# A hybrid three-branch encoder layer on one core: first weight loads fenced behind the first pieces' scaling, products placed between states and outputs, and planner holds lengthened

## The chip, the cores and the metric

The kernel runs on one core of one Trainium2 chip. The metric is the device time of one execution in microseconds (us), lower is better; the time before is the median of three executions, 756.55 us (756.28 to 756.60). All times below are microseconds unless marked otherwise. The engines are called PE (TensorE, the matrix engine), DVE (VectorE), ACT (ScalarE), POOL (GpSimd) and SP (SyncE, which here only issues transfers).

## The reference, cut to what matters

One layer reads x (1024 frames of 1024 numbers), normalises each frame, projects it to 16 segments, runs three linear-attention branches of four heads each side by side (HGRN2, GLA, mLSTM), norms and gates each head, and projects the 1536 concatenated columns back, with a residual and a last norm.

```python
def reference(x, norm_w, w_in, b_in, ...):
    h = _rmsnorm(x, norm_w[l])
    parts = _split_columns(h @ w_in[l] + b_in[l])
    y_hg = _gated_head_norm(_hgrn2_branch(parts, lower_bounds[l]), parts["hg_z"], hg_norm_w[l])
    y_gla = _gated_head_norm(_gla_branch(parts, gla_w_a2[l], gla_b_a2[l]), parts["gla_z"], gla_norm_w[l])
    y_ml = _gated_head_norm(_mlstm_branch(parts, ml_conv_w[l], ml_conv_b[l]), parts["ml_z"], ml_norm_w[l])
    y = jnp.concatenate([y_hg, y_gla, y_ml], axis=-1)
    x = x + y @ w_out[l]
    return _rmsnorm(x, final_norm_w)
...
def step(state, inp):            # one chunk of a gated linear attention head
    b = jnp.cumsum(gc, axis=2)
    att = jnp.einsum("bhtd,bhsd,bhtsd->bhts", qc, kc, dec)   # dec: pairwise decays, causal
    out = einsum(att, vc) + einsum(qc * jnp.exp(b), state)
    state = jnp.exp(b_last) * state + einsum(kc * jnp.exp(b_last - b), vc)
```

GLA's decays come from a small second projection: `log_sigmoid(parts["gla_a"] @ w_a2 + b_a2) / 16`. mLSTM's gates are two columns a head, with a running maximum.

## The kernel before

**Arithmetic.** Every product is made in three passes: an operand is split into a high part in a reduced fp32 format and a low remainder, and PE multiplies high by high, low by high, and high by low into the same accumulator bank. Such a triple with 512 moving columns is the unit of the projections (lines 346 to 348). `load_w` (line 220) fetches one block of weights: a transfer on SP into a `wraw` buffer (two of them), the high part by a copy on ACT (line 230, `whi`), the low part by a subtraction on DVE (line 231, `wlo`); both have four buffers.

**Start.** `proj_first` projects the first three pieces (f0, q0, z0 of HGRN2 head 0) in six accumulator banks while x arrives. The frames' scales are applied afterwards: `row_sums` and `row_scale` bring them across with PE transposes, ACT copies them into RSB (line 276), and DVE multiplies the six banks by RSB (line 339), which frees the banks. The next product, the pass over v0 (line 379, 280 columns: v0, the mLSTM gates and the GLA gate input), needs two of these banks. Its outputs are scaled on DVE (line 406).

**The planner.** From there on a class `Weave` interleaves chains (Python generators) with the stream of projections on PE. A chain yields `(cost, delay)` or `(cost, delay, tag, held)`: PE is taken to be busy for `cost`, the chain may go on `delay` later, and the accumulator slot of kind `tag` is taken to be free `held` later. These guesses alone decide where small products stand in PE's order, which is fixed when the program is built; the other engines' orders follow from a scheduler and are fixed too. Each engine works through its queue in order.

**The chains that the change touches.** For each half of a head: `radix4` (line 441, two levels of decays with 48-column products at line 462, copied out of bank `pt` at line 467) and `tree` (lines 491 and 522); then `tail` runs `states` (transposes of K at line 573 to `kd` at 575, four products at 592, and a scan over chunks on DVE at 598, `S`), and `att_out` or `pair_out` (lines 607 to 640). The last row of the first half's output needs the last state of the second half (line 614, 640). `finish_half` squares the outputs on ACT (558), takes a power on POOL (217) and scales them on ACT (561), after which the `po` bank is free. `gates` makes the gate rows and, in `gla_alpha` (line 743), the GLA decays: pairs of products at line 750 into `po` banks, the second pair subtracted on DVE at 768. `ml_chain` (line 897) runs the mLSTM heads: `ml_states` (transposes, products at line 851, scan at 857) and `ml_out` (871 with the attention, 879 with the states).

**Sums.** `sum_steps` (line 1069) adds pairs of blocks of the output weights for a Strassen-like output product, one step after each projected piece: two transfers into the same two `wraw` buffers, an addition on DVE (line 1075), a store. The transfers of `load_w` and of these sums take turns in the two buffers.

Of the kernel before, what the change touches and what calls it, by code (L numbers as in the profile page):

```python
# [10 lines left out]
AF = mybir.ActivationFunctionType  # L11
# [125 lines left out]
def kernel(ctx: ExitStack, tc: tile.TileContext, x, xt, wt, wide, cols, vbias, wa2, wq, fw, masks, sel,  # L137
                      ident_in, out):
    nc = tc.nc
# [9 lines left out]
    po = ctx.enter_context(tc.tile_pool(name="po", bufs=2, space=PS))  # L149
# [10 lines left out]
    RSB = const.tile([128, T], F32, name="RSB")  # L160
# [56 lines left out]
        nc.gpsimd.tensor_tensor(dst, dst, mhalf[:, 0:dst.shape[1]], op=OP.pow)  # L217


    def load_w(src, cuts=None, raw=None, hilo=None):  # L220

        raw = wp.tile([128, 1024], F32, name="wraw", bufs=2) if raw is None else raw
        if hilo is None:
            hilo = [wp.tile([128, 1024], F32R, name=nm, bufs=4) for nm in ("whi", "wlo")]
        hi, lo = hilo

        def part(a, b):
            s = slice(a, b)
            nc.sync.dma_start(raw[:, s], src[:, s])
            nc.scalar.activation(hi[:, s], raw[:, s], AF.Copy)  # L230
            nc.vector.tensor_sub(lo[:, s], raw[:, s], hi[:, s].bitcast(F32))  # L231
        if cuts is None:
            part(0, src.shape[1])
            return hi, lo
        return (hi, lo), [lambda a=a, b=b: part(a, b) for a, b in zip(cuts, cuts[1:])]

# [34 lines left out]
    def row_scale():  # L271
        for half in range(2):
            p = ptr.tile([128, 512], F32, name="tp")
            for j in range(4):
                nc.tensor.transpose(p[:, j * 128:(j + 1) * 128], rs[:, 4 * half + j:4 * half + j + 1].to_broadcast([128, 128]), ident)
            nc.scalar.activation(RSB[:, 512 * half:512 * half + 512], p, AF.Copy)


    wide_w, scales, marks = [], [], []
# [1 line left out]
    def load_wide(i, hilo=None):  # L281
        k0, k1 = KSPLIT[i]
        t = load_w(wide[:, k0 * WIDE:k1 * WIDE], hilo=hilo)
        wide_w.extend((t, k - k0) for k in range(k0, k1))

    def proj_first(pieces):

        ws, loads = [], []
        for i in range(3):
            raw = fp.tile([128, 1024], F32, name="al", bufs=2) if i == 2 else None  # L290
            t, steps = load_w(wt[WIDX[pieces[i][0]]], WCUTS, raw)
            ws.append(t)
            loads.append(steps)
        ps = [[pl.tile([128, 512], F32, name=nm) for _ in range(2)] for pl, nm in ((pmain, "pm"), (po, "po"), (ptree, "pt"))]
        done = [0, 0, 0]

        def matmuls(i, k):
            hi, lo = ws[i]
            for kk in range(done[i], k):
                ks = slice(128 * kk, 128 * kk + 128)  # L300
                for half in range(2):
                    s = slice(512 * half, 512 * half + 512)
                    nc.tensor.matmul(ps[i][half], hi[:, ks], HI[kk][:, s], start=kk == 0, stop=False)
                    nc.tensor.matmul(ps[i][half], lo[:, ks], HI[kk][:, s], start=False, stop=False)
                    nc.tensor.matmul(ps[i][half], hi[:, ks], LO[kk][:, s], start=False, stop=kk == KC - 1)
            done[i] = k
        for k in range(KC):
            if k == 0:
                loads[0][0]()
            build_h(k, 2 if k < 2 else 1)  # L310
            if k == 0:
                loads[1][0]()
                loads[2][0]()
            for i in range(3):
                for a in range(1, len(WCUTS) - 1):
                    if (WORDER[i] + 2 * (a - 1)) == k:
                        loads[i][a]()
            if k >= 3:
                square(k - 3)
            if k < KOUT:  # L320
                for i in range(3):
                    matmuls(i, k + 1)
        for k in range(KC - 3, KC):
            square(k)
        load_wide(0, [fp.tile([128, 1024], F32R, name="al", bufs=2) for _ in range(2)])
        matmuls(0, KC)
        load_wide(1)
        matmuls(1, SUMS)
        mean = row_sums()
        matmuls(1, KC)  # L330
        load_wide(2)
        matmuls(2, SCALE)
        row_scale()
        matmuls(2, KC)
        with tc.issue_after(mean):
            load_consts()
        for (_, dst, evac), pp in zip(pieces, ps):
            for half in range(2):
                nc.vector.tensor_mul(dst(half), pp[half], RSB[:, 512 * half:512 * half + 512])
                evac(half)  # L340

    def nt_half(hi, lo, s):
        p = pmain.tile([128, 512], F32, name="pm")
# [97 lines left out]
    def radix4(Q, K, F, Kc, dA, l4, slack):  # L441

        g = 4 ** l4
        n = 128 // g
        Q4, K4, F4 = (a.rearrange("p (n j g) -> p n j g", j=4, g=g) for a in (Q, K, F))
        P = [F4[:, :, j, g - 1:g] for j in range(4)]
        over = lambda j0, j1: F4[:, :, j0:j1, g - 1:g].to_broadcast([128, n, j1 - j0, g])
        qm = wk.tile([128, 768], F32, name="qm")  # L450
        M = qm.rearrange("p (n j g) -> p n j g", j=6, g=g)
        nc.scalar.activation(qm.rearrange("p (n x) -> p n x", n=n)[:, :, 0:3 * g],
                             Q.rearrange("p (n x) -> p n x", n=n)[:, :, g:4 * g], AF.Copy)
        nc.vector.tensor_tensor(M[:, :, 3:5, :], Q4[:, :, 2:4, :], over(1, 3), op=OP.mult)
        marks.append(nc.vector.tensor_tensor(M[:, :, 5, :], M[:, :, 4, :], P[1].to_broadcast([128, n, g]), op=OP.mult).ins)
        yield 0.0, 4.0 + slack
        yield "pt"
        p = ptree.tile([128, 512], F32, name="pt")
        for c in range(4):
            for a in range(0, 128, 32):  # L460
                q = (4 * c + a // 32) * 48
                nc.tensor.matmul(p[a:a + 32, 48 * c:48 * c + 48], Kc[:, c, a:a + 32], qm[:, q:q + 48], start=True, stop=True)
        pm = p[:, 0:192].rearrange("p (m j g) -> p m j g", j=6, g=g)
        d4 = dA.rearrange("p c (m j g) -> p (c m) j g", j=4, g=g)
        for off, j, w in ((0, 0, 3), (96, 3, 2), (160, 5, 1)):
            mask = mk4[:, l4, off:off + 32 * w].rearrange("p (m j g) -> p m j g", j=w, g=g)
            nc.vector.copy_predicated(d4[:, :, 4 - w:4, :], mask, pm[:, :, j:j + w, :])
        nc.vector.tensor_tensor(Q4[:, :, 1, :], Q4[:, :, 1, :], P[0].to_broadcast([128, n, g]), op=OP.mult)
        nc.vector.tensor_tensor(Q4[:, :, 2:4, :], M[:, :, 3:6:2, :], P[0][:, :, None].to_broadcast([128, n, 2, g]), op=OP.mult)
        nc.vector.tensor_tensor(P[2], P[2], P[3], op=OP.mult)  # L470
        nc.vector.tensor_tensor(P[1], P[1], P[2], op=OP.mult)
        nc.vector.tensor_tensor(K4[:, :, 0:3, :], K4[:, :, 0:3, :], over(1, 4), op=OP.mult)
        marks.append(nc.vector.tensor_tensor(P[3], P[0], P[1], op=OP.mult).ins)
        yield 0.7, 1.9 + slack, "pt", 3.0 + slack

    def tree(Q, K, F, A, dA, nh, half, done, slack=0.0):

# [171 lines left out]
    def tail(w, heads, rows, Q, K, F, V, zs, yi, trees, ready, out_done):  # L649

        yield lambda: ready() and 0 in trees
        S = wk.tile([128, NC, 130], F32, name="S", bufs=1)
        Kc = K.rearrange("p (c t) -> p c t", c=NC)
        states_done, first = [], []
        for half in range(2):
            yield lambda: half in trees
            yield from states(Kc, V[0], F, list(zip(heads, rows)), S, half)
            yield 0.0, 2.2
            states_done.append(half)
            if len(heads) > 1:  # L660
                w.start(pair_out(att, Q, V[0], S, zs, yi, half, states_done, first, out_done))
                continue
            for i, h in enumerate(heads):
                yield lambda: len(zs) > i
                w.start(att_out(h, att[:, (yi + i) % 2], Q[:, i], V[0], S, zs[i], yi + i, half, states_done, first, out_done))
# [77 lines left out]
    def gla_alpha(r, als):  # L743
# [23 lines left out]
                s = slice(512 * half, 512 * half + 512)  # L767
                nc.vector.tensor_sub(al[:, s], ps[half], al[:, s])
        for half in range(2):
            yield 0.0, 0.0, "po", 2.0 + half  # L770
        nc.scalar.activation(al, al, AF.Exp, scale=1.0 / 16.0)
        als.append(al)

# [123 lines left out]
    def ml_chain(w, r, ready, PQK, Vs, ogs, gates, ys, zs, done):  # L897
# [22 lines left out]
        yield lambda: len(gates) == NC  # L920
        yield from ml_states(r, K, E, V, S, 1)
        states_of.append(r)
        yield from ml_out(r, Q, S, V, ogs[0], ys, 1, gates)
        for h in range(2):
            yield lambda: len(zs) > h
            for half in range(2):
                s = slice(512 * half, 512 * half + 512)
                dst = y_tile(4 + h)[:, 1] if r else ys[h]
# [263 lines left out]
    with tc.manual_schedule(engines={mybir.EngineType.PE}):  # L1192
# [87 lines left out]
        for c in range(4):  # L1280
            parts = [R] if c < 3 else [slice(512, 896), last]
            for n, cols in enumerate(parts):
                pc_ = slice(cols.start - 512, cols.stop - 512)
                p = ptree.tile([128, 512], F32, name="pt") if n else pa[c]
# [93 lines left out]
```

## Time and profile before

| | |
|---|---|
| median of three executions | 756.55 us |
| the profiled execution | 757.12 us, of which the core's span is 755.3 us |
| PE | 740.4 us busy, 98% of the span |
| PE weight loads | 619.6 us, under the products |
| DVE | 471.6 us, 62% |
| ACT | 353.2 us, 47% |
| POOL | 60.2 us, 8% |
| transfers | 80.58 MB, mean 107 GB/s |
| granted TensorE clock | 0.995 of full over the span |

PE is busy nearly all the time, so only what PE waits for, or does at the lower clock, can be gained. The list of PE's waits names the line that waited, the line on another engine that ended the wait, the sum, the number of times and the longest. A timeline row is a start, a length, an engine, a line, an operation with its tiles and shapes, a count, and in brackets the idle time ahead of it and what ended that. PE's lengths overlap, so its pace is read from one start to the next.

### The profile page before, as it was taken

The numbers are of one execution on the slowest core, as the hardware profiler recorded it, in microseconds if no ns is written. First come the engines' busy times: TensorE is split into PE (matmuls) and PEld (weight loads), VectorE is DVE, ScalarE is ACT, GpSimd is POOL, SyncE is SP. The second block draws the span as 40 slices with busy tenths as digits, with TensorE's granted clock in tenths as the row PEclk, the third lists the DMA queues.
The fourth block names the chain that finished last, engine by engine and source line by source line (L and its number), as shares of the span: only waits on it lengthen the run. The fifth ranks groups of instructions, "written<-read, shape, count | busy, mean of one in ns | idle before, by whom it ended". The sixth has DMA issues, their size and how long they took to land.

```text
span 755.3 us, 13831 instructions
## 1 busy us (share of the span) xinstructions
PE 740.4 (98%) x5550; PEld 619.6 (82%) x5550; DVE 471.6 (62%) x1004; ACT 353.2 (47%) x772; POOL 60.2 (8%) x107
## 2 busy tenths in 40 slices
PE   9999998999999999999999999999999999999996
PEld 7888886899887899788988878878877878888886
DVE  6987767766467538523662384353564358899864
ACT  6661577842343431544044553345270556454543
POOL 2000130010010020012001200101000110000011
PEclk9999999999999999999999999999999999999998
DMA  8443652332542232102020120031210077543323
GB/s 307 137 154 115 189 183 75 110 91 88 196 146 92 88 137 85 51 29 84 31 85 29 55 84 1 2 126 69 71 56 0 18 252 275 167 139 112 87 109 140
DMA packets 30545, 80.58 MB, mean 107 GB/s; under 512 B 3648, under 2 KB 7232, under 8 KB 30480
## 3 DMA queue, kind: packets, MB, share of 16 engines
q1 hardware_dynamic: 29664, 78.89, 31.3%
q8 instruction: 44, 0.72, 0.4%
q0 software_dynamic: 672, 0.53, 0.3%
q10 hardware_dynamic: 144, 0.26, 0.1%
q14 instruction: 21, 0.17, 0.1%
HBM read 63.74 MB, written 15.93 MB: 105 GB/s over the span
## 4 chain that ended last, share of the span: by engine, by line
PE 77%; ACT 7%; DVE 6%; DMA 6%; issue 1%; SPq 1%; POOL 0%; POOLq 0%; DVEq 0%; ACTq 0%
PE pm L346 10%; PE pm L348 10%; PE pm L347 9%; PE pm L398 4%; PE pm L379 4%; PE pm L400 4%; PE pm L399 4%; PE pm L380 3%; PE pm L381 3%; DMA wraw<-in_wt_dram 3%; DMA wraw<-in_wq_dram 2%; PE pm L1157 2%; PE pm L1158 2%; PE pm L1156 2%; DVE wlo L231 2%
## 5 line engine op out<-in xcount | busy, mean ns | idle before, releaser
L346 PE MATMUL pm<-hT,whi 128*128 128x512 f32 x400 | 163.5, 409 | 0.0
L348 PE MATMUL pm<-hT,wlo 128*128 128x512 f32 x400 | 156.8, 392 | 0.0
L347 PE MATMUL pm<-hT,whi 128*128 128x512 f32 x400 | 156.8, 392 | 0.0
L346 PEld LDWEIGHTS pm<-hT,whi 128*128 128x128 f32 x400 | 75.5, 189 | 16.9 <-issue 1.5
L348 PEld LDWEIGHTS pm<-hT,wlo 128*128 128x128 f32 x400 | 75.5, 189 | 16.7
L347 PEld LDWEIGHTS pm<-hT,whi 128*128 128x128 f32 x400 | 75.8, 189 | 13.6
L230 ACT ACTIVATE whi<-wraw 128x1024 fp32r<-128x1024 f32 (+4 forms) x47 | 45.7, 974 | 78.9 <-PE pm L347 31.7
L379 PE MATMUL pm<-whi,hT 128*128 128x256 f32 (+1 forms) x232 | 67.9, 293 | 0.0
L380 PE MATMUL pm<-wlo,hT 128*128 128x256 f32 (+1 forms) x232 | 66.0, 285 | 0.0
L381 PE MATMUL pm<-whi,hT 128*128 128x256 f32 (+1 forms) x232 | 66.0, 284 | 0.0
L231 DVE TENSOR_TENSOR wlo<-wraw,whi 128x1024 fp32r<-128x1024 f32 (+4 forms) x47 | 52.5, 1120 | 20.3 <-ACT whi L230 19.9
L406 DVE SCALAR_TENSOR_TENSOR big<-pm,rs,vb 128x256 f32<-128x256 f32 x72 | 30.9, 456 | 44.1 <-PE pm L400 27.3
L398 PE MATMUL pm<-whi,hT 128*128 128x512 f32 x128 | 52.5, 410 | 0.0
L400 PE MATMUL pm<-whi,hT 128*128 128x512 f32 x128 | 50.1, 392 | 0.0
L399 PE MATMUL pm<-wlo,hT 128*128 128x512 f32 x128 | 49.9, 390 | 0.0
L379 PEld LDWEIGHTS pm<-whi,hT 128*128 128x128 f32 x232 | 44.2, 190 | 0.8
L380 PEld LDWEIGHTS pm<-wlo,hT 128*128 128x128 f32 x232 | 44.3, 191 | 0.1
L381 PEld LDWEIGHTS pm<-whi,hT 128*128 128x128 f32 x232 | 44.2, 191 | 0.0
L533 ACT ACTIVATE att<-dc 32x128 f32<-32x128 f32 (+1 forms) x48 | 16.5, 343 | 54.8 <-DVE dc L513 54.3
L358 DVE TENSOR_TENSOR zg<-pm,RSB 128x512 f32<-128x512 f32 x22 | 15.2, 691 | 31.8 <-PE pm L348 26.7
L398 PEld LDWEIGHTS pm<-whi,hT 128*128 128x128 f32 x128 | 24.0, 188 | 7.7 <-issue 1.8
L400 PEld LDWEIGHTS pm<-whi,hT 128*128 128x128 f32 x128 | 24.0, 188 | 5.4
(391 smaller groups left out, 1502.4 us busy)
## 6 DMA issues: line engine op xcount, KB each, us to landing
wraw<-in_wt_dram SPq DMA_DIRECT2D x39, 512.0 KB, 3.8
wraw<-in_wq_dram SPq DMA_DIRECT2D x27, 512.0 KB, 3.6
wraw<-wsum SPq DMA_DIRECT2D x18, 512.0 KB, 3.5
wsum<-wraw SPq DMA_DIRECT2D x12, 512.0 KB, 2.9
big<-ydram SPq DMA_DIRECT2D x18, 256.0 KB, 5.4
ydram<-zg SPq DMA_DIRECT2D x8, 256.5 KB, 2.4
big<-in_xt_dram SPq DMA_DIRECT2D x4, 512.0 KB, 5.5
ydram<-zg SPq DMA_DIRECT2D x8, 255.5 KB, 2.6
```

Of the source, the lines that this page charges most:

```text
L230: nc.scalar.activation(hi[:, s], raw[:, s], AF.Copy)
L231: nc.vector.tensor_sub(lo[:, s], raw[:, s], hi[:, s].bitcast(F32))
L346: nc.tensor.matmul(p, hi[:, ks], HI[k][:, s], start=k == 0, stop=False)
L347: nc.tensor.matmul(p, hi[:, ks], LO[k][:, s], start=False, stop=False)
L348: nc.tensor.matmul(p, lo[:, ks], HI[k][:, s], start=False, stop=k == KC - 1)
L379: nc.tensor.matmul(p, HI[k][:, ts], hi[:, ks], start=k == 0, stop=False)
L380: nc.tensor.matmul(p, HI[k][:, ts], lo[:, ks], start=False, stop=False)
L381: nc.tensor.matmul(p, LO[k][:, ts], hi[:, ks], start=False, stop=k == KC - 1)
L398: nc.tensor.matmul(p, HI[k][:, ts], hi[:, ks], start=k == 0, stop=False)
L399: nc.tensor.matmul(p, HI[k][:, ts], lo[:, ks], start=False, stop=False)
L400: nc.tensor.matmul(p, LO[k][:, ts], hi[:, ks], start=False, stop=k == KC - 1)
L406: nc.vector.scalar_tensor_tensor(dst, p, rs[:, c:c + 1], b, op0=OP.mult, op1=OP.add)
```

## The change

Four things are changed. The copies and subtractions (ACT and DVE, not the transfers) of every later `load_w` without cuts are fenced behind the RSB copy and behind the last scaling of the first pieces. In `radix4` the slack is doubled in the second yield; it is 1.2 for head 0 alone, and 0 elsewhere. In `tail` the planner waits 3.2 instead of 2.2 between states and outputs, and in `ml_chain` a wait of 3.5 is put between the second half's states and its outputs. In `gla_alpha` the two banks of the second pair are held for 6 and 7 instead of 2 and 3.

```diff
+    evacuated = []
+
     def load_w(src, cuts=None, raw=None, hilo=None):
...
         if cuts is None:
-            part(0, src.shape[1])
+            with ExitStack() as fences:
+                for ins in evacuated:
+                    fences.enter_context(tc.issue_after(ins))
+                part(0, src.shape[1])
             return hi, lo
...
-            nc.scalar.activation(RSB[:, 512 * half:512 * half + 512], p, AF.Copy)
+            copy = nc.scalar.activation(RSB[:, 512 * half:512 * half + 512], p, AF.Copy)
+        return copy.ins
...
-        row_scale()
+        scale = row_scale()
...
-                nc.vector.tensor_mul(dst(half), pp[half], RSB[:, 512 * half:512 * half + 512])
+                mul = nc.vector.tensor_mul(dst(half), pp[half], RSB[:, 512 * half:512 * half + 512])
                 evac(half)
+        evacuated.extend((scale, mul.ins))
...
-        yield 0.7, 1.9 + slack, "pt", 3.0 + slack
+        yield 0.7, 1.9 + 2.0 * slack, "pt", 3.0 + 2.0 * slack
...
             yield from states(Kc, V[0], F, list(zip(heads, rows)), S, half)
-            yield 0.0, 2.2
+            yield 0.0, 3.2
...
-            yield 0.0, 0.0, "po", 2.0 + half
+            yield 0.0, 0.0, "po", 6.0 + half
...
         yield from ml_states(r, K, E, V, S, 1)
         states_of.append(r)
+        yield 0.0, 3.5
         yield from ml_out(r, Q, S, V, ogs[0], ys, 1, gates)
```

No product, addition or transfer is added or taken away. What moves is the order. In the changed kernel a line stands 2 lower up to `load_w`'s body and 5 to 9 lower behind it (line 614 becomes 621, 750 becomes 757, 879 becomes 886).

ACT after the last block of `proj_first`, before (L230 is the high part of a weight block, L276 the RSB copies, L950 the first gate's sigmoid):

```order
L230 ACTIVATE whi<-wraw 128x560
L230 ACTIVATE whi<-wraw 128x1024
L276 ACTIVATE RSB<-tp 128x512 x2
L950 ACT_TABLE_LOAD
L950 ACTIVATE f<-f,pc 128x512 x2
```

The same place on ACT now (L232, L281 and L958 are those lines):

```order
L232 ACTIVATE whi<-wraw 128x560
L281 ACTIVATE RSB<-tp 128x512 x2
L232 ACTIVATE whi<-wraw 128x1024
L958 ACT_TABLE_LOAD
L958 ACTIVATE f<-f,pc 128x512 x2
```

The copies go ahead of the block of 1024 columns; on DVE the subtraction of that block goes behind the six scalings in the same way.

DVE around the scan of head 0's second half, before (L598 is the scan, L231 a weight block's low part, L1075 a sum of output weights, L721 to L730 the gate rows, L454 to L471 the decays of head 1):

```order
L716 COPY big<-big 1x4x7
L598 SCALAR_TENSOR_TENSOR S<-S,f,pt 128x128
...
L726 TENSOR_SCALAR big<-big 32x128
L729 CAST big<-big 32x128 x2
L730 TENSOR_TENSOR big<-big 32x128 x2
L231 TENSOR_TENSOR wlo<-wraw,whi 128x1024
L739 COPY mcol<-tp 128x32
L358 TENSOR_TENSOR big<-pm,RSB 128x512
L1075 TENSOR_TENSOR wraw<-wraw 128x1024
L454 TENSOR_TENSOR qm<-big,f 128x128x2
```

The same place on DVE now, from the gate rows' last row to the scan's last (L605 is the scan, L233 the low part, L1083 the sum, L461 to L478 the decays of head 1):

```order
L737 TENSOR_TENSOR big<-big 32x128
L746 COPY mcol<-tp 128x32
L365 TENSOR_TENSOR big<-pm,RSB 128x512
L233 TENSOR_TENSOR wlo<-wraw,whi 128x1024
L461 TENSOR_TENSOR qm<-big,f 128x128x2
L462 TENSOR_TENSOR qm<-qm,f 128x128
L475 TENSOR_TENSOR big<-big,f 128x128
L477 TENSOR_TENSOR f<-f 128x128
L605 SCALAR_TENSOR_TENSOR S<-S,f,pt 128x128
L476 TENSOR_TENSOR big<-qm,f 128x128x2
L478 TENSOR_TENSOR f<-f 128x128
L605 SCALAR_TENSOR_TENSOR S<-S,f,pt 128x128 x2
L1083 TENSOR_TENSOR wraw<-wraw 128x1024
L605 SCALAR_TENSOR_TENSOR S<-S,f,pt 128x128
```

All seven steps of the scan stood ahead of the low part; now the last four stand behind it, behind the first decays of head 1, and the very last behind a sum.

PE at the mLSTM's second half, before (L851 states, L871 attention, L879 states into the outputs):

```order
L851 MATMUL pt<-big,kd 64x129 x6
L871 MATMUL po<-big,att 128x129 x4
L879 MATMUL po<-S,big 128x129 x4
```

The same place on PE now, in each of the two passes, ahead of the outputs (L353 to L355 is a projection triple, of which six follow the states):

```order
L858 MATMUL pt<-big,kd 64x129 x6
L353 MATMUL pm<-hT,whi 128x512
L354 MATMUL pm<-hT,whi 128x512
L355 MATMUL pm<-hT,wlo 128x512
...
L878 MATMUL po<-big,att 128x129 x4
L886 MATMUL po<-S,big 128x129 x4
```

Six triples now lie between the states and the outputs. Elsewhere on PE one triple or two more lie between a head's states and its outputs, and the chain of the gates moves forward: the first two products of line 750 stood side by side, 14 triples behind the block that begins with line 614; now the first stands 2 triples behind that block and the second 2 further.

## Rows read from the trace of the kernel before

**Rows 1.** PE's waits: engine, line and tile, what ended them; total, times, longest.

```profile
PE po L879 <- DVE S L857: 2.2, 2, 1.2
PE po L750 <- DVE al L768: 1.6, 1, 1.6
PE pm L379 <- DVE f L339: 1.5, 1, 1.5
...
PE pm L379 <- DVE big L406: 0.9, 2, 0.7
PE pt L462 <- DVE f L470: 0.5, 1, 0.5
...
PE po L640 <- DVE S L598: 0.4, 1, 0.4
```

**Rows 2.** Timeline of ACT, 36 to 43 us (the columns are told above).

```profile
39.96 1.06 ACT L230 ACTIVATE whi<-wraw 128x1024 fp32r<-128x1024 f32 x1 [3.57 <-DMA wraw<-in_wt_dram]
...
42.01 1.28 ACT L950 ACT_TABLE_LOAD   x1
```

**Rows 3.** Timeline of DVE, 41 to 107 us.

```profile
41.06 1.22 DVE L231 TENSOR_TENSOR wlo<-wraw,whi 128x1024 fp32r<-128x1024 f32 x1 [1.66 <-ACT whi L230]
...
72.80 0.63 DVE L406 SCALAR_TENSOR_TENSOR big<-pm,rs,vb 128x256 f32<-128x256 f32 x2 [0.91 <-PE pm L381]
73.74 1.30 DVE L231 TENSOR_TENSOR wlo<-wraw,whi 128x1024 fp32r<-128x1024 f32 x1 [0.31 <-ACT whi L230]
...
86.01 1.23 DVE L231 TENSOR_TENSOR wlo<-wraw,whi 128x1024 fp32r<-128x1024 f32 x1 [0.56 <-ACT whi L230]
...
90.84 1.23 DVE L1075 TENSOR_TENSOR wraw<-wraw 128x1024 f32<-128x1024 f32 x1 [0.74 <-DMA wraw<-in_wq_dram]
...
97.61 1.23 DVE L231 TENSOR_TENSOR wlo<-wraw,whi 128x1024 fp32r<-128x1024 f32 x1 [1.25 <-ACT whi L230]
...
105.13 0.51 DVE L454 TENSOR_TENSOR qm<-big,f 128x256 f32<-128x256 f32 x1 [1.37 <-ACT big L954]
...
106.38 0.40 DVE L470 TENSOR_TENSOR f<-f 128x128 f32<-128x128 f32 x1
```

**Rows 4.** Timeline of PE, 42 to 108 us.

```profile
42.94 0.40 PE L379 MATMUL pm<-al,hT 128*128 128x280 f32 x1 [1.53 <-DVE f L339]
...
72.59 0.40 PE L346 MATMUL pm<-hT,whi 128*128 128x512 f32 x1
...
95.99 0.38 PE L614 MATMUL po<-S,big 128*1 128x128 f32 x2
...
98.22 0.48 PE L346 MATMUL pm<-hT,whi 128*128 128x512 f32 x1
...
107.88 0.63 PE L750 MATMUL po<-RX,wa 96*128 96x512 f32 x2
```

**Rows 5.** Timelines of ACT, POOL and ACT: from squares to scaled outputs of head 0.

```profile
97.48 0.26 ACT L558 ACTIVATE sq<-po 128x128 f32<-128x128 f32 x1
...
99.40 1.05 POOL L217 TENSOR_TENSOR st<-st,mhalf 128x4 f32<-128x4 f32 x1
...
101.93 1.14 ACT L561 ACTIVATE osb<-po,st 128x128 f32<-128x128 f32 x4
```

**Rows 6.** Timeline of PE, 123 to 131 us.

```profile
123.14 0.39 PE L348 MATMUL pm<-hT,wlo 128*128 128x512 f32 x1
125.08 0.50 PE L750 MATMUL po<-RX,wa 96*128 96x512 f32 x1 [1.56 <-DVE al L768]
125.52 0.45 PE L491 MATMUL pt<-big 128*32 128x16 f32 x32
...
126.69 0.78 PE L346 MATMUL pm<-hT,whi 128*128 128x512 f32 x1
...
130.22 0.39 PE L348 MATMUL pm<-hT,wlo 128*128 128x512 f32 x1
```

**Rows 7.** Busy time (and instructions) of PE, PEld, DVE, ACT, POOL; granted clock, DMA share, GB/s.

```profile
120.00:140.00 20.00, 18.44 (x223) 14.24 (x212) 13.53 (x40) 14.81 (x24) 0.35 (x1) 0.91 0.09 28
```

## The prediction

> **What bounds the kernel now.** The table of engines comes first: PE is busy 98% of the span, the others far less, and no product is added or taken away. So the time can only move by what PE waits for and by what it does at the lower clock. The list of PE's waits [rows 1] is therefore the list of what can be won: 2.2 before the mLSTM's outputs with states (line 879, two waits), 1.6 before the GLA gates (750), 1.5 before the pass over v0 (379), 0.9 inside that pass, 0.5 at head 1's decays (462), 0.4 at the last rows of a pair (640). The timelines of PE, ACT and DVE around each of them tell who is late. The brackets leave out a little: from the product at 123.14 to the one at 125.08 there are 1.94, where a product starts 0.23 after the one before, so this wait costs 1.7, not 1.56 [rows 6]; I add 0.15 to each wait. The 0.23 is from the stretch 98.22 to 107.88, 14 triples in 9.66, 0.69 a triple [rows 4]. Behind the wait at 125.08 PE starts eight products between 126.69 and 130.22, in 3.53 instead of 1.84: 1.7 lost, in the only stretch of which the granted clock is low, 0.91 between 120 and 140 [rows 6, 7].
>
> Since all orders are fixed, the second thing to read is the order itself: each engine works through its queue, so an instruction that is put behind another one cannot start before it. I follow the path from the start and set each new place against the durations of the rows.
>
> **Term a, the start.** The copies into RSB stood behind a high part of 1.06 that itself waited 3.57 for its block [rows 2]; the scalings waited in part behind the low part, which waited 1.66 for that high part [rows 3]. With the fence both go first, and the wait of 1.53 before the pass over v0 [rows 4] goes. What is late next is the low part of the block of v0's successor and the outputs of the pass: line 406 still makes PE wait (0.9 in all, [rows 1]), and the sigmoid's table load, 1.28 [rows 2], moves forward by only about 1.0, since one high part of 1.06 stays ahead of it. So the bounds are −1.0 (the pass ends as the sigmoids allow) and −2.4 (both waits go, 1.5 + 0.9); I take −1.6, nearest to the one wait that surely goes, 1.53. Call the end of that pass E; before it was 72.59 [rows 4].
>
> **Term b, the scan of head 0's second half.** In the new order of DVE the last four steps of the scan stand behind a low part, behind the first decays of head 1, and the very last behind a sum (line 1075). Line 614 on PE needs the last one. The low part cannot come sooner than its block: the two buffers are filled in turn, and the low parts at 73.74, 86.01 and 97.61 are 12.27 and 11.60 apart [rows 3]. That one starts 25.0 after E, less some 0.3 because the one at 73.74 waits 0.31 for its high part: E + 24.6. On ACT, behind the high part of that block (done when the low part starts), come a copy of 512 columns, a table load and the 512 columns of line 954: 0.6 + 1.28 + 0.7, the tiles estimated from 1.06 for 1024 columns [rows 2]. So line 454 on DVE starts at E + 27.1. From 454 to the end of 470 there were 1.65 (105.13 to 106.78, [rows 3]); then a scan step, two tiles of the decays (0.7), two scan steps, the sum (1.2) and the last step. A scan step has the tile of line 470, 0.40, as its upper end; I take 0.33. That makes 28.75 + 0.33 + 0.7 + 0.66 + 1.2 + 0.35 = E + 32.0. PE reaches line 614 on its own at 23.4 (72.59 to 95.99, [rows 4]) plus what is put ahead of it, six triples and two groups of line 491 that leave the pass, 4.8 in all: E + 28.2. **+3.8**. The lower end is 2.5 (the sum's operands early and the decays at the speed of their shortest tiles); nothing hides it, as PE has nothing else in its queue ahead of 614.
>
> **Term c, the gates of GLA.** Line 750 takes the two `po` banks in turn. Before, its first product stood 14 triples behind the block of line 614 (98.22 to 107.88) and found a free bank; now it stands 2 triples behind. The bank comes free when line 561 has scaled head 0's first half. Behind 614 that takes 0.3 for the product, then from the squares at 97.48 to the end of POOL's power at 100.45, 2.97, then 1.14 for 561 [rows 5] and about 0.4 of handing over: 4.8. PE has 2.23 of work from 95.99 to 98.22 [rows 4] and two triples, 1.4: it waits 1.2. The second product needs the other half's bank: a square, a power of 1.05 with its handover, a copy and a high part (1.06) on ACT, and again 1.14, against 0.3 and two triples on PE: some 1.75 more. **+3.0**; bounds 0 (the first half's bank is scaled before the scan has ended, since only one row of it needs the last state) and 4.5 (all of ACT's high part lies in between twice).
>
> **Term d, what is won for it.** As PE is later by b and c while DVE and ACT go on, head 1's decays are ready (0.5 + 0.15) and so is the gates' second pair, 750 at 125.08 (1.7): both waits go. Without that wait I expect the lower clock behind it to go too, 1.7. Together **−4.1**. In exchange the groups of line 491 behind 750 now wait for copies on ACT that have a high part (1.06) and two tiles ahead of them: 0 if the new waits have covered it, 1.6 if nothing does; I take **+0.7**.
>
> **Term e, the rest.** Line 640 gets a triple or two of cover (0.69 each) for a wait of 0.5: it goes. The two waits of 879 get six triples each, 4.1, against at most 1.2 + 0.15: both go, 2.5. **−3.0**. Here the cover is paid from the projections that follow, which stand in the program anyway; the outputs move back by 4.1, and the heads behind them are far from the end of the span. I expect no new wait there, as no wait of that stretch is in rows 1 apart from these.
>
> **Sum.** −1.6 + 3.8 + 3.0 − 4.1 + 0.7 − 3.0 = −1.2. The profiled execution takes 757.12, its span 755.3 and 1.8 around it, so the changed kernel's profile should take 755.9. The profiled execution lies 0.57 above the median of the runs; I take that off: 755.3.
>
> **Rivals.** *The edits do what they look like* (call it clean): the scheduler's order on DVE costs nothing, because the scan's inputs come in good time and the block that I put at E + 24.6 is there far earlier; b and c are nought and all waits of rows 1 go. −1.6 − 4.1 − 3.0 = −8.7 or a little less: 748 to 750. For it: the cover added is in each place larger than the wait. Against it: the 12 between low parts [rows 3] is a row, and the order of DVE and PE is read off the program.
>
> *The early losses are larger*: c and the 0.7 of d at their upper ends, 4.5 and 1.6, give −1.2 + 1.5 + 0.9 = +1.2: 757.7, no change. For it: ACT carries high parts of 1.06 between all the small tiles.
>
> *Slower: the clock falls at the new waits.* The trace shows one fall to 1.2 GHz, behind a wait of 1.56 followed by narrow products, for 1.7 [rows 6, 7]. The new waits at 614 and 750, of 3.8, 1.2 and 1.75, stand close together among products of 128 columns. If each long one brings one such stretch, the sum grows by 1.7 a fall: one fall gives 757.0, two give 758.7. So it decides from the second fall on. Against it: the wait of 1.53 at 42.94 [rows 4] has no low stretch behind it. The Trainium skill, in "TensorE: Matmul & The Clock Gate", section "What's actually happening", says that the throttled clock is the default state and that only activity releases it. By that rule a place with several waits in a row is where the clock should fall; the trace agrees for the one at 125.08 and not for the one at 42.94.
>
> **How the numbers follow.** A measurement of this kernel can tell a change of about 0.2% from none, so "same" is 755.04 to 758.06. The forecast has a chance of 0.50, with an own range of 753.5 to 756.8 (a between −1.0 and −2.4, b down to 2.5, the handovers of c); its middle lies beside the lower edge of the band, so it gives 0.25 to faster and 0.25 to same. Clean has 0.20, all faster. Larger losses have 0.15: 0.12 same and 0.03 slower. The falling clock has 0.15: 0.14 slower and 0.01 same. That makes 0.45 faster, 0.38 same, 0.17 slower. The range of 750.5 to 758.5 leaves out a part of clean (about 0.10) and of the falls beyond the second (about 0.08).
>
> **What would show it.** a: no wait before 379, while 406 still makes PE wait a little. b: a wait of PE at line 614 (621 in the changed kernel) for the scan, of 2.5 to 4, and in DVE's timeline the low part, the decays and the sum ahead of the last steps. c: two waits at 750 (757) that ACT's line 561 (568) ends. d: no wait at 462, none at the second pair of 750, no stretch of the lower clock there, a short wait at 491. e: no waits at 640 and 879. The prediction is wrong if 614 does not wait, for then the time is nearer 749; if the granted clock is below 0.95 in more than one stretch of 20 us, for then it is 757 or more; or if the output product at the end waits for blocks that it did not wait for before, which I price at nothing.

## The result and the profile after

The changed kernel takes 766.92 us (median of three executions, 764.65 to 769.02) against 756.55: 1.4% slower, a ratio of 1.0137 (95% interval 1.0091 to 1.0184). The profiled execution has a span of 762.9. The prediction of 755.3 (750.5 to 758.5) missed it; the loss is in the output product, which the prediction priced at nothing.

PE's waits in the changed kernel (engine, line and tile, what ended them; total, times, longest); they answer to [rows 1]:

```profile
PE po L1164 <- ACT whi L1115: 5.9, 1, 5.9
PE po L621 <- DVE S L605: 2.0, 1, 2.0
PE tp L949 <- DVE al L946: 1.5, 1, 1.5
PE pt L498 <- DVE dc L474: 1.0, 1, 1.0
PE po L757 <- ACT osb L568: 1.0, 1, 1.0
PE po L633 <- ACT osb L568: 0.8, 2, 0.4
PE tp L580 <- DVE big L536: 0.8, 1, 0.8
PE pm L386 <- DVE big L413: 0.6, 2, 0.4
PE po L1165 <- DVE wlo L1116: 0.5, 1, 0.5
PE pt L529 <- ACT att L532: 0.4, 1, 0.4
```

All waits of [rows 1] but those inside the pass over v0 (now line 386) are gone, 621 and 757 wait, though less than forecast, and one wait is larger than any of before: line 1164, the first product of the output stage that needs a fresh block of output weights. The chain that ended last, followed back from there, names the cause (start, length, engine, tile, line):

```profile
634.77 0.63 ACT zg L437
635.45 14.39 POOL zg L439
650.76 6.08 DMA wraw<-in_wq_dram
656.86 1.06 ACT whi L1115
657.94 1.24 DVE wlo L1116
659.22 0.80 PE po L1165
```

Line 439 copies one column of a gate tile (128 x 1) on POOL. It took 14.38 us here; in the kernel before (line 432) it took 0.49, at 636.95. POOL's row, then SP's queue, in the changed kernel (start, length, operation, count, idle time before):

```profile
635.45 14.38 POOL L439 COPY zg<-zg 128x1 f32<-128x1 f32 x1 [7.55 <-ACT zg L437]
```

```profile
649.86 0.80 SPq L1213 DMA_DIRECT2D zg<-in_x_dram  x2
650.76 0.38 SPq L1114 DMA_DIRECT2D wraw<-in_wq_dram  x1
```

SP is to load rows of x into that gate tile's buffer, so it waits for the copy, and the block of weights stands behind it in the same queue. It is issued at 650.76, where the kernel before issued its block at 644.81. What DVE did meanwhile (same columns; part of its stream, which has no idle time from 634.19 to 649.79):

```profile
634.19 3.09 DVE L1147 TENSOR_TENSOR big<-big 128x512 f32<-128x512 f32 x5
...
637.80 2.49 DVE L1136 TENSOR_TENSOR hT<-big,hT 128x512 fp32r<-128x512 f32 x4
...
648.50 1.29 DVE L1136 TENSOR_TENSOR hT<-qm,hT 128x512 fp32r<-128x512 f32 x2
657.94 1.23 DVE L1116 TENSOR_TENSOR wlo<-wraw,whi 128x1024 fp32r<-128x1024 f32 x1 [8.15 <-ACT whi L1115]
```

The copy ends at 649.83, 0.04 behind the last instruction of that stream. It lay over 23 instructions of DVE, from one that ended 0.03 behind its start to that last one, all with two operands in SBUF.

### The profile page after: what moved, and what is told of

It reads as the page before. It is cut to its first block, busy times and chain, and to the rows that moved or that the text cites. A ratio compares the mean times of both kernels' runs of the same rounds, so it can differ in the third digit from the quotient of the medians.

```text
span 762.9 us, 13820 instructions
## 1 busy us (share of the span) xinstructions
PE 741.4 (97%) x5550; PEld 618.8 (81%) x5550; DVE 470.8 (62%) x1004; ACT 355.5 (47%) x774; POOL 77.1 (10%) x107
## 4 chain that ended last, share of the span: by engine, by line
PE 82%; DVE 6%; ACT 5%; DMA 3%; POOL 2%; issue 1%; SPq 0%; POOLq 0%; DVEq 0%; ACTq 0%
PE pm L353 11%; PE pm L354 10%; PE pm L355 10%; PE pm L405 4%; PE pm L407 4%; PE pm L406 4%; PE pm L386 4%; PE pm L387 3%; PE pm L388 3%; POOL zg L439 2%; DMA wraw<-in_wq_dram 2%; PE pt L529 1%; PE pt L599 1%; DMA wraw<-in_wt_dram 1%; PE pt L498 1%; PE tp L573 1%
## 5 line engine op out<-in xcount | busy, mean ns | idle before, releaser
L353 PE MATMUL pm<-hT,whi 128*128 128x512 f32 x400 | 163.0, 408 | 0.0
L355 PE MATMUL pm<-hT,wlo 128*128 128x512 f32 x400 | 156.4, 391 | 0.0
L353 PEld LDWEIGHTS pm<-hT,whi 128*128 128x128 f32 x400 | 75.2, 188 | 16.9 <-issue 1.8
L355 PEld LDWEIGHTS pm<-hT,wlo 128*128 128x128 f32 x400 | 75.1, 188 | 16.5
L232 ACT ACTIVATE whi<-wraw 128x1024 fp32r<-128x1024 f32 (+4 forms) x47 | 45.6, 973 | 80.3 <-PE pm L388 32.4
L233 DVE TENSOR_TENSOR wlo<-wraw,whi 128x1024 fp32r<-128x1024 f32 (+4 forms) x47 | 52.5, 1118 | 22.9 <-ACT whi L232 22.4
L386 PEld LDWEIGHTS pm<-whi,hT 128*128 128x128 f32 x232 | 44.2, 191 | 0.8
L388 PEld LDWEIGHTS pm<-whi,hT 128*128 128x128 f32 x232 | 44.3, 191 | 0.0
L216 POOL TENSOR_SCALAR st<-st 128x4 f32<-128x4 f32 x24 | 7.9, 329 | 284.1 <-ACT sq L565 283.8
L439 POOL COPY zg<-zg 128x1 f32<-128x1 f32 x12 | 18.4, 1530 | 180.6 <-ACT zg L437 180.6
L565 ACT ACTIVATE sq<-po 128x128 f32<-128x128 f32 x64 | 17.7, 277 | 30.0 <-PE po L647 14.2
```

Of the source, the lines that this page charges most:

```text
L353: nc.tensor.matmul(p, hi[:, ks], HI[k][:, s], start=k == 0, stop=False)
L355: nc.tensor.matmul(p, lo[:, ks], HI[k][:, s], start=False, stop=k == KC - 1)
L386: nc.tensor.matmul(p, HI[k][:, ts], hi[:, ks], start=k == 0, stop=False)
L388: nc.tensor.matmul(p, LO[k][:, ts], hi[:, ks], start=False, stop=k == KC - 1)
L439: nc.gpsimd.tensor_copy(z[:, 0:1], z[:, T:T + 1])
```

## The experiments

**Is it the copy?** e1 takes this one copy off POOL; the orders of PE, DVE and SP stay the same.

```diff
-                nc.gpsimd.tensor_copy(z[:, 0:1], z[:, T:T + 1])
+                (nc.scalar.copy if name == "mz3" else nc.gpsimd.tensor_copy)(z[:, 0:1], z[:, T:T + 1])
```

> The changed kernel with one instruction moved: the last of the twelve one-column copies of a gate tile (line 439, 14.4 us long on POOL in the changed kernel's profile) is done on ACT; the orders of PE, DVE and SP stay. Theory A (the copy was held up because DVE's back-to-back instructions with two SBUF inputs keep the port that POOL needs, SP's queue stood behind it, and the weight block behind that): PE's wait of 5.9 us at line 1164 goes, the time is 755 to 756.5. Rival B (the block of output weights is late because of SP's order, whatever the copy does): the wait stays over 4 us and the time stays over 763.

Measured: the wait at 1164 is gone, 758.5 us, ratio 1.0021 (1.0010 to 1.0031). A holds for the wait, B falls. The time is 2 above the upper end of what was expected of A; this is taken up below.

e3 makes the same edit in the kernel before.

> The kernel before with the same one copy moved to ACT, where it took 0.49 us on POOL. Theory A: nothing waits for it there, so 756.5, no change. Rival (the move itself gains something by another way): under 755.

Measured: 756.49, ratio 1.000 (0.9991 to 1.0009). The move gains nothing by itself.

**Is it DVE's stream that holds the copy?** e2 leaves it on POOL and puts seven short memsets into DVE's stream (in the output stage a few instructions of DVE and ACT change places by it):

```diff
             low = nc.vector.tensor_sub(lo, raw, hi.bitcast(F32))
+            if i == 1:
+                with tc.issue_after(low.ins):
+                    low = nc.vector.memset(gap, 0.0)
         lows.append(low.ins)
```

> The changed kernel with the copy left on POOL, and short memsets put into DVE's stream of the output product (one in each set of six low parts, the first after the copy's start about 3.5 us behind it). Theory A: the copy ends with the first memset, 3 to 5 us long instead of 14.4, the wait at the output product (line 1164 of the changed kernel) goes, 755 to 757. Rival C (POOL's copy waits for something else than DVE, a transfer or its own queue): still over 10 us long, over 763.

Measured: 757.93, ratio 1.0018 (1.0009 to 1.0028), no wait at the output product; as in e1 the time lies above A's range. POOL in e2 (line 440 is the copy):

```profile
637.01 3.69 POOL L440 COPY zg<-zg 128x1 f32<-128x1 f32 x1 [7.55 <-ACT zg L438]
```

It ends at 640.70, and DVE's first memset behind its start begins at 640.63: the copy was let in there, after seven instructions with two operands. C falls.

**Does every program suffer?** e7 and e8 keep the copy on POOL in two other orders: only the fence and the mLSTM's wait of 3.5 (e7), and all edits but the doubled slack (e8).

> The same kernel as e4 with all gate columns copied on POOL as in the changed kernel. If every program in which the last copy meets the output product's DVE stream loses as the changed kernel does: copy over 10 us, time over 761. If it depends on the moment at which the copy comes, as the kernel before (0.49 us) lets expect: copy under 1 us and 753.3, as e4; times of both kinds among the executions would show that chance decides in each.

> The same kernel as e5 with all gate columns copied on POOL. As for e7: either the copy takes over 10 us and the time is over 763, or under 1 us and 755.3 as e5.

Measured: e7 762.67 (762.39 to 762.77), ratio 1.0081 (1.0066 to 1.0096), with the copy's row

```profile
632.78 14.38 POOL L439 COPY zg<-zg 128x1 f32<-128x1 f32 x1 [7.55 <-ACT zg L437]
```

and e8 765.27 (one execution), with

```profile
634.53 14.39 POOL L439 COPY zg<-zg 128x1 f32<-128x1 f32 x1 [7.55 <-ACT zg L437]
```

So three of the orders tried here hold it, and the kernel before does not. In each it is one or the other: e7's four executions lie between 762.39 and 762.77, while the 52 of the kernel before that ran beside the experiments lie between 755.27 and 757.99, so none of them can have lost what a held copy costs. With the copy on ACT the same two orders take 753.26 (e4) and 755.34 (e5): the held copy costs 9.4 and 9.9 us there, and 8.4 in the changed kernel (766.92 against e1's 758.5).

**What holds it?** Four probes compute no part of the layer. The first sets ten copies each against several streams of DVE.

> No part of the layer is computed; only DVE, ACT and POOL run. In seven sections POOL makes ten copies of one column, one about every 2 us, while DVE runs 48 instructions on 128x512 back to back: none; sums of two SBUF tiles; sums of a PSUM and an SBUF tile; one-input operations; sums of two SBUF tiles with a memset after every eighth; sums of two SBUF tiles against memsets on POOL; sums of two SBUF tiles again. Theory A: against sums of two SBUF tiles the first copies last up to the end of the stream (over 10 us), with the memsets up to the next memset (up to 5 us), and 0.2 to 0.7 us in the sections with none and with PSUM, and for POOL's memsets. Rival D (POOL gets in at the next end of a DVE instruction): at most 0.9 us in every section.

POOL's copies in it (operation, count, duration in ns as smallest/median/largest, first and last start). No stream, sums of two SBUF tiles, sums of a PSUM and an SBUF tile, operations with one SBUF input, memsets on POOL:

```profile
L177 POOL COPY col_none<-v x10: 183/183/184, 7.2 to 23.8; 128x1 f32<-128x1 f32 x10
...
L177 POOL COPY col_two<-v x10: 194/593/758, 26.3 to 42.9; 128x1 f32<-128x1 f32 x10
...
L177 POOL COPY col_psum<-v x10: 183/183/184, 55.3 to 71.9; 128x1 f32<-128x1 f32 x10
...
L177 POOL COPY col_one<-v x10: 177/178/14012, 84.1 to 100.7; 128x1 f32<-128x1 f32 x10
...
L175 POOL MEMSET col_memset<- x10: 98/98/99, 132.9 to 151.6; 128x1 f32 x10
```

Against two SBUF operands a copy waits, but here only for the end of the instruction that is running (0.76 at most), as D said; so it does in the two sections that are not shown, with memsets in DVE's stream (0.20 to 0.30) and in the repeat of the sums (0.20 to 0.76). Against one-input operations, which A did not name, the first copy waited 14.01 us, to the end of the stream, so D falls too. Against PSUM operands, and for POOL's memsets, there is no wait. So for two SBUF operands A's rule is too strong: to be held is possible, not certain. The Trainium skill, "SBUF — State Buffer", section "SBUF: two separate sides", says that DVE and GpSimd (POOL) share one pair of ports, that an operation of DVE in a two-port mode, or with two SBUF inputs against a GpSimd operation that reads SBUF, has the pair for the whole instruction if it starts first, and that the other one is blocked. The probe agrees for two SBUF inputs (0.19 to 0.76), for a PSUM input (0.18) and for POOL's memsets (0.10); whether the one-input operations ran in a two-port mode, no run shows. In the changed kernel the blocked copy was passed over at the ends of 22 instructions in a row.

The second probe moves the copy's start by a few ns a time (some 13 in the trace), since in the changed kernel, e2, e7 and e8 it came 48 to 61 ns behind the start of an instruction, and in the kernel before 243.

> No part of the layer is computed. POOL copies a column 66 times in each of three sections, its start moving by about 9 ns against DVE's stream from copy to copy, while DVE runs 192 instructions on two SBUF tiles back to back, a memset after every 48: sums into a third tile, differences into one of the two operands, low parts (fp32r out). Theory E (POOL gets in at the end of an instruction, except when it arrives some 45 to 60 ns behind the start of one, in the overlap with the one before, as in the changed kernel and in e2; then it waits for the next memset): one or a few copies of 5 to 30 us in each section, the others at most 0.8 us. Theory F (it is the kind of instruction, not the moment): all copies of the sections with differences or low parts long, none with sums. Rival G (neither): all at most 0.8 us.

```profile
L173 POOL COPY v_two<-v_two x66: 183/197/24946, 9.8 to 140.6; 128x1 f32<-128x1 f32 x66
...
L173 POOL COPY v_self<-v_self x66: 183/384/688, 143.3 to 261.7; 128x1 f32<-128x1 f32 x66
...
L173 POOL COPY v_lowpart<-v_lowpart x66: 183/292/542, 264.3 to 382.7; 128x1 f32<-128x1 f32 x66
```

One copy of 198 was held, 24.95 us, to the first memset; those queued behind it followed one by one. (Some of the 198 came behind the end of a stream, and the third section's stream had gaps, so this is no count of chances.) It started 474 ns behind the start of an instruction, while others at 475 and 478, and two at 47, were let in. E and F fall. The held one was POOL's first, behind 9.40 us of rest, which gave the third probe: one copy a stretch.

> No part of the layer is computed. In 24 stretches DVE runs 24 instructions on two SBUF tiles back to back (14 us), and POOL, idle before for over 10 us, makes one copy in the middle, at another moment in each stretch. Theory H (a copy after a long pause of POOL is the one that is kept out): nearly all last to the end of the stretch, over 5 us. Theory C (chance of the moment): a few of the 24 do, the rest stay under 0.8 us. Rival G (it takes something that only the layer's stream has): none does.

```profile
L167 POOL COPY z<-z x24: 418/11896/12166, 10.2 to 345.5; 128x1 f32<-128x1 f32 x24
```

21 of 24 were held to the end of the stretch (10.0 to 12.2 us), at moments from 3 to 449 ns behind the start of an instruction; three took 0.42 to 0.66. That is near H. But the copy of a stretch started some 3 us after the held copy of the stretch before had ended, so the rest ahead of it was mostly short: the name "pause" does not fit. Nor does the last section of the first probe, whose first copy was let in behind 9.97 us of rest. The three were the 9th, 15th and 21st of the 24, evenly spaced, which does not look like chance. The fourth probe changes what POOL does ahead of the copy.

> No part of the layer is computed. As in p3, one POOL copy in the middle of each of 32 stretches of 24 back-to-back DVE instructions on two SBUF tiles; what POOL did before it changes: nothing for over 10 us; a memset directly ahead of the copy; four memsets, about one a us; a copy done just before DVE's stretch began, some 3 us earlier. Theory H (a pause of POOL alone decides): the copies behind a pause are held to the end of their stretch (about 10 us) in most of 8, those behind memsets and behind the earlier copy last under 0.8 us. Theory H2 (only a copy that was itself let in a short while before helps): those behind memsets are held too. Theory C (chance): the four kinds do not differ.

```profile
L180 POOL COPY z_pause<-z_pause x8: 10046/12028/12355, 10.2 to 420.2; 128x1 f32<-128x1 f32 x8
...
L180 POOL COPY z_one_memset<-z_one_memset x8: 215/396/719, 23.2 to 434.9; 128x1 f32<-128x1 f32 x8
...
L180 POOL COPY z_memsets<-z_memsets x8: 11691/11951/12276, 37.8 to 449.5; 128x1 f32<-128x1 f32 x8
...
L180 POOL COPY z_copy_before<-z_copy_before x8: 200/395/712, 52.8 to 464.5; 128x1 f32<-128x1 f32 x8
```

Eight of eight held with nothing ahead, none with one memset of the same tile directly ahead, eight of eight with four memsets of another tile, the last of them just as close, none with a copy 2.3 to 3.0 us ahead. C falls: it is not chance. H falls with the four memsets. H2 would have the copies behind the single memset held too, unless the held copy that ended 2.3 to 2.9 us ahead of it counts, and p3's held copies had such a one ahead as well. The four kinds always came in the same order, so what the stretch before left behind is not separated from what POOL did directly ahead. What decides whether a copy is let in stays open, and with it why the kernel before's copy, after 11.72 us of rest, was let in.

**What would the edits have brought?** e4 keeps the fence and the mLSTM's wait only; e5 all but the doubled slack; e6 is e4 with the longer hold of the banks. All have the last copy on ACT. The edits undone are, for e4:

```diff
-        yield 0.7, 1.9 + 2.0 * slack, "pt", 3.0 + 2.0 * slack
+        yield 0.7, 1.9 + slack, "pt", 3.0 + slack
...
-            yield 0.0, 3.2
+            yield 0.0, 2.2
...
-            yield 0.0, 0.0, "po", 6.0 + half
+            yield 0.0, 0.0, "po", 2.0 + half
```

> Only the fence at the start and the wait of 3.5 in the mLSTM chain are kept (slack, 3.2 and the banks' hold as before); the last gate column is copied on ACT. By terms a and f of the prediction: no wait before the pass over v0 (1.9 less), no wait at the mLSTM's outputs (2.5 less), all else as before: 752.2, 751.5 to 753. Rival (what is gained early is taken back at the next wait, so that only one of the two counts): 754 to 755.

> The changed kernel without the doubled slack in radix4, the last gate column copied on ACT; to be compared with e1 (758.5). Theory: it is the doubled slack that puts the gates' products of line 757 forward and the scan's last steps behind a low part and a sum; without it the waits at 621 and 757 go, the old wait of 1.7 before the gates' second pair comes back: 752 to 754. Rival 1 (the 3.2 between states and outputs does it): no change against e1, 758. Rival 2 (the waits only move to the next product that needs the same DVE queue): 756 to 757.

> Fence, the mLSTM's wait of 3.5 and the longer hold of the banks; slack and 3.2 as before, the last gate column on ACT. The hold puts some five triples (3.4 us) more between the gates' first and second pair than in e4. Theory: the wait of 1.7 that e4 still has at line 757 for the subtraction goes, and nothing else changes: 751.5 (751 to 752). Rival (the wait moves to lines 498 or 529, whose inputs come from the same DVE queue): 753, as e4.

Measured: e4 753.26 (752.55 to 753.69), ratio 0.9958 (0.9944 to 0.9972), the shortest time of all kernels here. (The prediction has no term f: meant is the mLSTM's part of its term e, 2.5; its term a was 1.6.) Both count, so the rival falls. The medians show 3.0 of the 4.4 expected. Product by product against the profile of the kernel before, which ran 0.57 above its median, both are whole: e4 is 1.5 early behind the pass over v0 and 4.2 early behind the mLSTM's outputs. A wait of 1.4 at line 529 is new in it:

```profile
PE po L757 <- DVE al L775: 1.6, 1, 1.6
...
PE pt L529 <- DVE big L536: 1.4, 1, 1.4
```

e5: 755.34, ratio 0.9989 (0.9978 to 1.0000), against 1.0021 for e1: the doubled slack costs 0.32%, 2.4 us. Rival 1 falls, but the time lies between the theory's and rival 2's: the wait at 621 goes, 757 still waits 1.9 for line 568. e6: 755.93, ratio 0.9995 (0.9984 to 1.0005), above both forecasts: the wait at 757 goes and comes back in front of products that wait for the same DVE queue, as the rival said, but larger, and the most of it at a line that it did not name (580):

```profile
PE tp L580 <- DVE big L536: 3.3, 1, 3.3
PE pt L498 <- DVE dc L474: 2.0, 2, 1.7
```

## Why the prediction was wrong

I follow PE by its projection products, whose order is the same in both kernels, and compare the times at which the same one starts, at places where the same small products lie behind it in both.

**Up to the output product it was right in sum.** A product of the output stage shortly ahead of its wait starts at 645.07 where before it started at 646.23: 1.2 earlier, as forecast. The steps:

- a, right: the pass over v0 starts at 41.06 instead of 42.94 [rows 4], and a product behind its end at 78.36 instead of 79.75, 1.4 earlier (forecast 1.6).
- b, mechanism right, its parts not: just behind the block with 621 PE is 2.0 late (104.42 against 102.44), so the stretch cost 3.4 (forecast 3.8). But the wait at 621 is 2.0, below the 2.5 to 4 that was named as its sign; waits of 0.77 at 580 and 0.36 at 599, which were not priced, make up most of the rest. The pass over v0 ends at 69.46 (E). The last scan step ends at 102.24, E + 32.8 (forecast 32.0), and PE could have started 621 at E + 30.8 (forecast 28.2). DVE's timeline has the order that was read off, with the sum ahead of the last step:

```profile
97.71 0.52 DVE L461 TENSOR_TENSOR qm<-big,f 128x256 f32<-128x256 f32 x1 [1.30 <-ACT big L962]
...
100.77 1.22 DVE L1083 TENSOR_TENSOR wraw<-wraw 128x1024 f32<-128x1024 f32 x1
101.90 0.34 DVE L605 SCALAR_TENSOR_TENSOR S<-S,f,pt 128x128 f32<-128x128 f32 x1
```

- c, mechanism right, size wrong: 1.3 instead of 3.0 (PE is then 3.3 late, 118.15 against 114.89). The first product of 757 waits (0.96 in the bracket, forecast 1.2); the second, 1.72 later, does not, so its term of 1.75 was nought:

```profile
107.01 0.50 PE L757 MATMUL po<-RX,wa 96*128 96x512 f32 x1 [0.96 <-ACT osb L568]
108.73 0.40 PE L757 MATMUL po<-RX,wa 96*128 96x512 f32 x1
```

- d, half of what was forecast: 1.8 won (148.27 against 146.77 is 1.5 late) instead of 3.4. The gains are there: no wait at 469, none at the second pair of 757, and the granted clock of the changed kernel's profile is 1.00 between 120 and 140, where it was 0.91 [rows 7]. The exchange was too small: 498 and 529 wait 1.05, 0.4 and 0.3, from start to start 2.2 instead of 0.7.
- e, right: 640 and 879 (647 and 886) wait no more, 3.2 (forecast 3.0). Not priced: a wait of 0.4 at 592 that goes, 0.7 from product to product, and two waits of 633 for a bank that come, 1.3.

c was 1.7 too dear, d 1.6 too good, and the unpriced waits made up the rest; the agreement of the sum is partly luck.

**The clock's 1.7 in term d was not there to be won.** e4 shows it, with the same wait at 757 as the kernel before [rows 6] and no low clock behind it. First e4, then the kernel before:

```profile
123.59 0.50 PE L757 MATMUL po<-RX,wa 96*128 96x512 f32 x1 [1.55 <-DVE al L775]
...
136.38 1.32 PE L529 MATMUL pt<-big 128*64 128x64 f32 x16 [1.39 <-DVE big L536]
```

```profile
138.04 1.15 PE L522 MATMUL pt<-big 128*64 128x64 f32 x16
```

From the waiting product to that group it takes 12.79 in e4 and 12.96 in the kernel before (from 125.08). At the higher clock PE comes to the group earlier and waits there for DVE (L529 of the changed kernels is L522 of the one before). The executions agree. Where no copy was held to the end of DVE's stream, the profiles with a stretch of 0.91 between 80 and 140 have a mean granted clock of 0.994 to 0.996 (before, e1, e2, e3, e5), and those without 0.997 (e4, e6). Of the 52 executions of the kernel before, the 21 up to 0.996 have a median of 756.51 and the 31 from 0.997 one of 756.48.

**The step that failed** is the one that priced the output product at nothing. It cost 8.4 (from 1.2 early to 7.2 late, which then stays to the end): 5.94 and 0.46 of waits, the products in between, and a low clock behind them. The windows of the changed kernel, early and there (busy time and instructions of PE, PEld, DVE, ACT, POOL; granted clock, DMA share, GB/s):

```profile
100.00:120.00 20.00, 17.04 (x147) 13.51 (x145) 12.40 (x30) 15.74 (x37) 2.85 (x5) 1.00 0.35 119
120.00:140.00 20.00, 18.38 (x231) 13.82 (x229) 13.54 (x45) 17.12 (x26) 0.19 (x1) 1.00 0.12 41
...
640.00:660.00 20.00, 13.60 (x57) 10.59 (x56) 11.85 (x18) 4.99 (x8) 9.83 (x1) 0.87 0.33 105
660.00:680.00 20.00, 20.00 (x87) 16.43 (x86) 20.00 (x33) 11.61 (x20) 0.00 (x0) 0.96 0.41 132
```

The rows of before gave no price for it. The copy took 0.2 to 0.6 us wherever it stood; nothing in the trace of before said that it can take 14. What could be seen, and was not looked for, is the chain: a tiny POOL instruction inside a dense stretch of DVE, SP behind it, and the output weights behind SP. The prediction named a wait of the output product as what would make it wrong, and no mechanism for it.

**The rest: the slower rival was half right.** Without the held copy the change gives 757.9 (e2) and 758.5 (e1), not 755.3. Between 80 and 120 the profiles of both have a stretch of 1.2 GHz behind a new wait, and the changed kernel's own profile has none there: e1 behind 621, e2 (0.91 between 80 and 100) behind a wait of 1.84 at 581, the 580 of the others. e1, its wait and its window:

```profile
103.01 0.38 PE L621 MATMUL po<-S,big 128*1 128x128 f32 x2 [2.13 <-DVE S L605]
...
106.55 0.69 PE L353 MATMUL pm<-hT,whi 128*128 128x512 f32 x1
```

```profile
100.00:120.00 20.00, 17.01 (x139) 13.72 (x139) 10.86 (x23) 14.00 (x34) 2.44 (x4) 0.91 0.32 109
```

In e1 the clock falls behind the wait for the scan, over products of 128 columns, and one fall was priced at 757.0. Here it does cost: the eight executions of e1 with a mean granted clock of 0.994 to 0.996 took 758.03 to 759.90, the two with 0.997 and 0.999 took 756.71 and 756.48. Those two are still 1.2 to 1.4 above the forecast of 755.3, about what the clock's 1.7 was to bring. The forecast assumed that the old fall goes and no new one comes. That comes about in some executions and not in others: in the changed kernel's profile the same wait of 2.0 has no fall behind it, and e4's wait of 1.6 at 757 is followed by none where the kernel before has one [rows 6]. What decides that is not shown. So the whole change, copy aside, loses 0.2%, and its two clean parts are worth 0.42% (e4).

## What to carry to other kernels

Before a change of order is priced, follow the queues that are shared by unlike work: here a one-column copy on POOL stood between SP and the weights, and all three new orders that left it there with DVE's stream as it was exposed it. A copy on POOL that reads SBUF should not stand in front of a transfer that matters while DVE runs a dense stream with two SBUF operands; ACT did it with no measurable cost (e3). Cover that is bought by putting other products forward is lost again where their inputs come late: the fence and the mLSTM's wait gained, the doubled slack put a scan and the gates' products behind work of DVE and ACT and lost 2.4. And a wait or a low clock that goes is worth no more than the way to the next wait for another engine: the fall behind [rows 6] hid a wait of 1.4.

## What was not expected of the hardware

A POOL copy of 128 x 1, 0.18 us alone, can last as long as DVE's uninterrupted stream: 14.38 us over 23 two-operand instructions in the layer, 24.95 us in a probe, 14.01 us against one-input operations in another, and a single DVE memset lets it in (3.69 us in e2). With the same stream, 8 of 8 or none of 8 copies were held, depending on the kind of stretch; which property of it decides was not found.
